# Encoder trunk on one core: ten warming products behind a memset of their own, and a weight's low part moved ahead of the last row sums' low parts

## The chip, the cores and the metric

The kernel runs on one core of one Trainium2 chip. The metric is the device time of one execution in microseconds (us). Before the change the median of three runs is 1899.04 us (1897.82, 1899.04 and 1899.11).

## What is computed

The reference is an encoder of two layers over 512 tokens of width 1024, in float32. Each layer adds three terms to the residual x, each computed from a root-mean-square norm of x:

```
x += 1/2 * SwiGLU(norm(x))                            feed-forward 1, inner width 2816
x += W_o( g_na * NA(h) W_na + g_f * FNet(h) W_f )     mixer, h = norm(x), gates g = sigmoid(h W + bias)
x += 1/2 * SwiGLU(norm(x))                            feed-forward 2
```

NA is attention with 8 heads of 64 over bands of keys with a relative bias; FNet is the real part of a 2-D Fourier transform of another projection of h. A last norm follows the second layer.

## The kernel before, in words

Every product is made in three matmuls on parts of the operands: a value is split into a high part, a rounded copy that ACT makes, and a low part, the value minus its high part, that DVE makes; then come high by high, high by low and low by high. Many large products are also cut into quarters by Strassen's scheme, so seven block products named 1 to 7 stand for eight.

**Weights.** They come as granules of 128x1024 floats, in an order written out in `stage_items`. `Stream` walks through them: a granule is fetched by a DMA of SP several places ahead (with a second, adding DMA of POOL for a summed quarter), and `prep` makes its parts. ACT copies `raw` into `whi` (line 178, or 173 with the sign turned), DVE subtracts to give `wlo` (line 181, or 174). `whi` and `wlo` have three buffers each. `ws.prep(to)` issues these for all granules up to `to`; `ws.next(ahead)` hands out the granule at `ws.pos` and prepares `ahead` more.

**The front.** Lines 129 to 135: DVE sets `ones` and `warm`, ACT runs one Tanh on `ones` so that its table is loaded, and writes the result into a column of `warm`; PE then runs `WARM` products of `warm` by itself, whose result nobody reads. They are followed by the first real block, `cl`: for each of eight tiles of the input, `given` (line 345 on) makes `xh` on ACT (L303), `xr` (L352) and `xl` (L304) on DVE from a tile `xt` that SP fetches and `gn` that ACT's queue fetches; PE multiplies by `whi` with `xh` and `xl` (L470, L471) for four blocks of tokens and then by `wlo` (L473).

**Attention's end.** In `stage_mixer` the order of DVE's and ACT's instructions is written out by hand (a `manual_schedule` block): each of the two engines keeps the order of the program text there, and PE's order is left to the scheduler outside of the inner blocks. At the end of the block stand the last two of eight attention steps, 6 and 7. `att_pv` makes their weighted sums on PE (`ps` from `p` and `v` or `vs`), `att_split` splits each sum into `o` (high on ACT, L1284; low on DVE, L1287), two instructions a step on each engine. The tile `o` of the last pair of heads is the last quarter of the contraction of the output product `fill(o, ns, 0, w)`: 48 matmuls at L294, L295, L296 that use two granules, called here the first and the second; `fill` runs three quarters of two row blocks before it needs the last quarter.

**What comes behind it.** The gates' first Strassen products are prepared in a second hand-ordered block. `minus` gives `t12` in three DVE steps: two differences (L1416) and their sum (L1418). ACT copies `t12` (`high`, L1641, tile t1h), then `ws.prep(ws.pos + 3)` makes the first granule of block product 1 (L173 on ACT, L174 on DVE). DVE goes on with L1416, t1l (L1646), two more additions into `t12` (L1656), L1416; ACT copies `t12` again (L1641, t2h), DVE makes t2l, and then comes the second granule of product 1 (L173, L174), the copies of `fill`'s results (L1313) and the granules of product 5 (L178, L181). PE runs product 1 into `A` (L470, L471, L473), then product 5 into `B`. Each engine takes its instructions strictly in its own order.

The stage occurs once in each of the two layers, with the same text.

Of the kernel before, what the change touches and what calls it, by code (L numbers as in the profile page):

```python
# [9 lines left out]
F32 = mybir.dt.float32  # L10
# [3 lines left out]
AF = mybir.ActivationFunctionType  # L14
# [3 lines left out]
P = 128  # L18
# [8 lines left out]
NH, DH = 8, 64  # L27
EPS = 1e-6
NEG = -1.0e30
WARM = 9  # L30
AHEAD = 2
ORDER = (1, 5, 2, 6, 7, 3, 4)
FETCH = 8
# [56 lines left out]
def encoder_kernel(  # L90
# [3 lines left out]
    V, S, G, PE = nc.vector, nc.scalar, nc.gpsimd, nc.tensor  # L94

    cp = ctx.enter_context(tc.tile_pool(name="cp", bufs=1))
    sp = ctx.enter_context(tc.tile_pool(name="sp", bufs=1))
# [8 lines left out]
    def nm(s):  # L106
        uid[0] += 1
        return f"{s}_{uid[0]}"

    def slot(dt=F32, s="k", shape=(4, 256)):  # L110
        return kp.tile([P, *shape], dt, tag="k", name=nm(s), bufs=23)

    def hilo(s):
        t = slot(F32R, s, (2, T))
        return t[:, 0, :], t[:, 1, :]

    def bank(s="ps"):
        return pp.tile([P, T], F32, tag="ps", name=nm(s))
# [7 lines left out]
    idents = cp.tile([P, 2, P], F32, tag="ident", name="ident")  # L126
    ident, mirror = idents[:, 0, :], idents[:, 1, :]
    ones = cp.tile([P, 1], F32, tag="ones", name="ones")
    V.memset(ones, 1.0)
    warm = slot(BF16, "warm", (T,))  # L130
    V.memset(warm, 0.0)
    S.activation(warm[:, 0:1], ones, AF.Tanh)
    pw = bank()
    for _ in range(WARM):
        PE.matmul(pw, warm[:, 0:P], warm, start=True, stop=True)
# [120 lines left out]
    class Stream:  # L256
# [27 lines left out]
        def next(self, ahead=AHEAD):  # L284
            self.prep(self.pos + 1 + ahead)
            it = self.items[self.pos]
            self.pos += 1
            return it.out

    ws = Stream()  # L290
    raw_pool = [None]

    def mm3(ps, lh, ll, rh, rl, start, stop, again=False):
        PE.matmul(ps, lh, rh, start=start, stop=False, skip_group_check=again)  # L294
        PE.matmul(ps, lh, rl, start=False, stop=False, skip_group_check=again)  # L295
        PE.matmul(ps, ll, rh, start=False, stop=stop, skip_group_check=again)  # L296
# [680 lines left out]
    def stage_mixer(l, norm, nxt):  # L977
# [288 lines left out]
        def att_pv(i, p_):  # L1266
            hp, pr = divmod(i, 2)
            po = bank()
            hs = slice(hp * P, (hp + 1) * P)
            for jj in range(2):  # L1270
                ph, pl = p_[jj]
                for c in range(2):
                    vh, vl = vch[BAND[2 * pr + jj] + 2 * c]
                    cs = slice(c * 256, (c + 1) * 256)
                    mm3(po[:, jj * 256 : jj * 256 + 256], vh[:, hs], vl[:, hs], ph[:, cs], pl[:, cs], c == 0, c == 1)
            return po

        def att_split(i, po):
            hp, pr = divmod(i, 2)
            pv = po.rearrange("p (a e q) -> p a e q", a=2, e=2)  # L1280
            oh, ol = [z[:, pr * 256 : pr * 256 + 256].rearrange("p (a q) -> p a q", a=2) for z in o[hp]]
            for e in range(2):
                r = slice(64 * e, 64 * e + 64)
                S.activation(oh[r], pv[r, :, e, :], AF.Copy)  # L1284
            for e in range(2):
                r = slice(64 * e, 64 * e + 64)
                V.tensor_tensor(ol[r], pv[r, :, e, :], oh[r].bitcast(F32), ALU.subtract)  # L1287


        def rows_of(src, tb, w, kts=range(4), ps=None):  # L1290

            ps = bank() if ps is None else ps
            t = slice(tb * P, (tb + 1) * P)
            for kt in kts:
                h_, l_ = src[kt]
                wh, wl = w[kt // 2]
                c = slice((kt % 2) * T, (kt % 2 + 1) * T)
                mm3(ps, h_[:, t], l_[:, t], wh[:, c], wl[:, c], kt == 0, kt == 3)
            return ps
# [112 lines left out]
        def minus(p, q, s):  # L1412

            t = [slot(F32, s), slot(F32, s)]
            for z in range(2):
                V.tensor_tensor(t[z], p[z], q[z], ALU.subtract)  # L1416
                yield t
            V.tensor_tensor(t[0], t[0], t[1], ALU.add)  # L1418
            yield t

        def f_copy(i, tb, ps, by_act=False):

            if tb % 2 == 0:
                fs[i, tb // 2] = slot(F32, "fs", (2, T))
            to = fs[i, tb // 2][:, tb % 2, :]
            if by_act:
                S.activation(to, ps, AF.Copy)
            else:
                V.tensor_copy(to, ps)

        first_f = []
        with tc.manual_schedule(engines={mybir.EngineType.DVE, mybir.EngineType.Activation}):
            with tc.manual_schedule(engines={mybir.EngineType.PE}):
# [179 lines left out]
                first = minus(B[0, 0], B[0, 1], "t1")  # L1613
# [14 lines left out]
                pt_[7] = [h() for h in ph]  # L1628
                ws.prep(ws.pos + 1)
                f_copy(1, 3, rows_of(yf, 3, second_f), True)  # L1630
                t12, _ = next(first)
                o.append(hilo("o"))
                po = [att_pv(i, pt_.pop(i)) for i in (6, 7)]
                att_split(6, po[0])
                att_split(7, po[1])
        ws.prep(ws.pos + 2)
        acts = {1: (hx[0], lx[0], 0), 2: (hx[1], lx[1], 0), 3: (hx[1], lx[1], 256), 4: (hx[0], lx[0], 256)}

        def high(src, s):
# [138 lines left out]
    for l in range(L):  # L1778
        nxt = Norm(3 * l + 1)
        stage_ffn(norm, nxt, False)  # L1780
        norm, nxt = nxt, Norm(3 * l + 2)
        stage_mixer(l, norm, nxt)
        norm, nxt = nxt, Norm(3 * l + 3)
        stage_ffn(norm, nxt, l == L - 1)
        norm = nxt
# [139 lines left out]
```

## Time and profile before

| what | value |
|---|---|
| median of the runs | 1899.04 us |
| the profiled execution's own time | 1898.17 us |
| its span, first to last instruction | 1896.4 us |
| time around the span | 1.77 us |
| TensorE clock granted, mean | 0.999 |
| DVE busy | 1647.8 us (87%) |
| ACT busy | 1189.4 us (63%) |
| DMA | 372.74 MB, mean 197 GB/s |

The profile is of one execution. In a row of the timeline the columns are the start (us from the span's start), the duration, engine, line, operation, tiles (output, then inputs), shape, and in brackets the idle time of the engine ahead of the instruction with what released it. PE stands for matmuls, PEld for the loads of their stationary operand, which overlap with the matmul before. A matmul's duration contains its filling and draining: what counts for a chain of matmuls is the distance from start to start.

### The profile page before, as it was taken

To read this page: it belongs to the slowest core of one execution; us is meant where nothing else is said; L and a number is where in the kernel's file an instruction comes from. 1 tells how busy PE (TensorE), PEld (TensorE's weight loads), DVE (VectorE), ACT (ScalarE), POOL (GpSimd) and SP (SyncE) were. 2 spreads that over 40 slices of the span, in tenths; PEclk is the share of its full clock that TensorE was granted. 3 is DMA by queue.
4 is the path that set the end of the run, shared out by engine and by line. 5 is a ranking of instruction groups with operands and counts; after the bars stand their busy time and mean duration, and the time that the engine had idled before them with its cause. 6 is when DMAs were issued, how large, how long until landed. Compare 5 with 4: busy or idle time off the path is not lost.

```text
span 1896.4 us, 25088 instructions
## 1 busy us (share of the span) xinstructions
PE 1884.2 (99%) x9149; PEld 1579.3 (83%) x9149; DVE 1647.8 (87%) x2006; ACT 1189.4 (63%) x1700; POOL 171.5 (9%) x210
## 2 busy tenths in 40 slices
PE   9999999999999999999999999999999999999998
PEld 7888888888888888888888888888888888888886
DVE  7877899788989977889997778998989899887898
ACT  6655665668666755566665556666685576556664
POOL 0101011100111011001010100101001101100010
PEclk9999999999999999999999999999999999999999
DMA  9777498932886777649877664988248767766594
GB/s 302 202 201 194 148 247 265 225 106 97 248 218 165 183 188 205 175 154 263 250 184 213 185 181 152 268 273 204 84 139 238 206 167 179 207 175 178 173 283 137
DMA packets 106939, 372.74 MB, mean 197 GB/s; under 512 B 12288, under 2 KB 12416, under 8 KB 106816
## 3 DMA queue, kind: packets, MB, share of 16 engines
q1 hardware_dynamic: 78144, 272.80, 41.9%
q0 software_dynamic: 28528, 98.33, 28.4%
q8 instruction: 71, 1.16, 0.2%
q14 instruction: 52, 0.43, 0.1%
q10 hardware_dynamic: 144, 0.02, 0.0%
HBM read 365.85 MB, written 2.11 MB: 194 GB/s over the span
## 4 chain that ended last, share of the span: by engine, by line
PE 98%; DVE 1%; issue 0%; ACT 0%; DVEq 0%; ACTq 0%
PE A L470 10%; PE A L471 10%; PE A L473 10%; PE o L470 7%; PE o L473 7%; PE o L471 7%; PE B L470 5%; PE B L471 5%; PE B L473 5%; PE ps L295 4%; PE ps L294 4%; PE ps L296 3%; PE C L471 2%; PE C L470 2%; PE C L473 2%; PE tr L593 2%
## 5 line engine op out<-in xcount | busy, mean ns | idle before, releaser
L178 ACT ACTIVATE whi<-raw 128x1024 fp32r<-128x1024 f32 (+1 forms) x536 | 553.6, 1037 | 387.1 <-PE A L471 123.4
L181 DVE TENSOR_TENSOR wlo<-raw,whi 128x1024 fp32r<-128x1024 f32 (+1 forms) x536 | 636.2, 1193 | 167.7 <-ACT whi L178 166.1
L149 POOL DMA_DIRECT2D raw<-in_wst_dram x166 | 144.4, 895 | 1375.5 <-DMA raw<-in_wst_dram 846.1
L163 DVE TENSOR_TENSOR raw<-raw,raw 128x1024 f32<-128x1024 f32 (+1 forms) x150 | 177.5, 1191 | 1.2
L471 PE MATMUL A<-whi,xl 128*128 128x512 f32 x400 | 155.7, 389 | 0.0
L470 PE MATMUL A<-whi,xh 128*128 128x512 f32 x400 | 155.7, 389 | 0.0
L473 PE MATMUL A<-wlo,xh 128*128 128x512 f32 x400 | 115.1, 389 | 0.0
L173 ACT ACTIVATE whi<-raw 128x1024 fp32r<-128x1024 f32 (+1 forms) x83 | 85.8, 1036 | 43.0 <-PE o L471 12.8
L174 DVE SCALAR_TENSOR_TENSOR wlo<-raw,whi 128x1024 fp32r<-128x1024 f32 (+1 forms) x83 | 98.0, 1195 | 13.1 <-ACT whi L173 13.1
L675 ACT ACTIVATE th<-sn,rh 128x512 f32<-128x512 f32 x80 | 56.9, 714 | 69.2 <-DVE sn L545 69.2
L540 ACT ACTIVATE sn<-A 128x512 f32<-128x512 f32 x104 | 60.7, 588 | 46.4 <-PE A L473 46.3
L473 PEld LDWEIGHTS A<-wlo,xh 128*128 128x128 f32 x400 | 75.1, 188 | 15.6
L471 PEld LDWEIGHTS A<-whi,xl 128*128 128x128 f32 x400 | 75.1, 188 | 15.4
L470 PEld LDWEIGHTS A<-whi,xh 128*128 128x128 f32 x400 | 75.1, 188 | 15.4
L470 PE MATMUL C<-whi,xh 128*128 128x512 f32 x208 | 81.1, 390 | 0.0
L471 PE MATMUL C<-whi,xl 128*128 128x512 f32 x208 | 81.0, 389 | 0.0
L471 PE MATMUL B<-whi,xl 128*128 128x512 f32 x208 | 81.0, 389 | 0.0
L470 PE MATMUL B<-whi,xh 128*128 128x512 f32 x208 | 80.9, 389 | 0.0
L473 PE MATMUL C<-wlo,xh 128*128 128x512 f32 x208 | 59.8, 389 | 0.0
L473 PE MATMUL B<-wlo,xh 128*128 128x512 f32 x208 | 59.8, 389 | 0.0
L470 PE MATMUL B<-whi,t5h 128*128 128x512 f32 x136 | 54.2, 399 | 0.0
L695 DVE TENSOR_TENSOR at<-at,at 128x1024 f32<-128x1024 f32 (+1 forms) x48 | 53.8, 1130 | 0.0
(446 smaller groups left out, 4783.9 us busy)
## 6 DMA issues: line engine op xcount, KB each, us to landing
raw<-in_wst_dram SPq DMA_DIRECT2D x470, 512.0 KB, 5.3
raw<-in_wst_dram POOLq DMA_DIRECT2D x174, 512.0 KB, 8.0
raw<-in_wst_dram SPq DMA_DIRECT2D x30, 256.0 KB, 3.9
bm<-in_bias_dram SPq DMA_DIRECT2D x16, 384.0 KB, 3.8
vs<-v SPq DMA_DIRECT2D x12, 256.0 KB, 3.8
x<-in_xin_dram SPq DMA_DIRECT2D x4, 512.0 KB, 10.2
raw<-in_wst_dram POOLq DMA_DIRECT2D x8, 256.0 KB, 8.1
dft<-in_dft_dram POOLq DMA_DIRECT2D x8, 256.0 KB, 4.2
```

The lines of the kernel that those rows point to most:

```text
L149: G.dma_start(out=self.t, in_=wst[GRAN_AT[self.plus]][:, 0 : self.n], accum_op=ALU.add)
L163: V.tensor_tensor(self.raw.t, self.raw.t, self.add.t, ALU.add)
L173: S.activation(hi, t, AF.Copy, scale=-1.0)
L174: self.last = V.scalar_tensor_tensor(lo, t, -1.0, hi.bitcast(F32), ALU.mult, ALU.subtract)
L178: S.activation(hi[:, cs], t[:, cs], AF.Copy)
L181: self.last = V.tensor_tensor(lo[:, cs], t[:, cs], hi[:, cs].bitcast(F32), ALU.subtract)
L294: PE.matmul(ps, lh, rh, start=start, stop=False, skip_group_check=again)
L295: PE.matmul(ps, lh, rl, start=False, stop=False, skip_group_check=again)
L470: PE.matmul(ps, lh, rh, start=start, stop=False, skip_group_check=again)
L471: PE.matmul(ps, ll, rh, start=False, stop=False, skip_group_check=again)
L473: PE.matmul(ps, lh, rl, start=False, stop=stop, skip_group_check=again)
L540: S.activation(t[:, b, :], ps[b], AF.Copy)
```

## The change

It has two parts.

- **Front.** `warm` is set first and `ones` second on DVE; ACT's Tanh writes into a small tile of its own instead of a column of `warm`; there are ten warming products instead of nine.
- **Attention's end.** The sum that finishes `t12` (L1418 on DVE) moves from ahead of steps 6 and 7 to behind their splits, as the last line of the hand-ordered block; and `ws.prep(ws.pos + 2)`, which makes the second granule of `fill`, moves from behind the block to a place ahead of the two splits and inside the block.

```diff
-WARM = 9
+WARM = 10
...
-    V.memset(ones, 1.0)
     warm = slot(BF16, "warm", (T,))
     V.memset(warm, 0.0)
-    S.activation(warm[:, 0:1], ones, AF.Tanh)
+    V.memset(ones, 1.0)
+    S.activation(sp.tile([P, 8], F32, tag="sq", name=nm("sq"), bufs=2)[:, 0:1], ones, AF.Tanh)
...
                 ws.prep(ws.pos + 1)
                 f_copy(1, 3, rows_of(yf, 3, second_f), True)
-                t12, _ = next(first)
                 o.append(hilo("o"))
                 po = [att_pv(i, pt_.pop(i)) for i in (6, 7)]
+                ws.prep(ws.pos + 2)
                 att_split(6, po[0])
                 att_split(7, po[1])
-        ws.prep(ws.pos + 2)
+                t12, _ = next(first)
```

The order of instructions on each engine that results, at attention's end (numbers count the granules):

```
DVE before: wlo 1 | L1418 | o x4 | wlo 2        | L174 | L1416 | t1l | L1656 x2 | L1416 | t2l | L174
DVE after:  wlo 1 | wlo 2 | o x4 | L1418        | L174 | L1416 | t1l | L1656 x2 | L1416 | t2l | L174
ACT, both:  whi 1 | fs | whi 2 | o x4 | t1h | L173 | t2h | L173 | L1313 x4 | L178 x2
```

On PE the 48 matmuls of `fill` change places among themselves: before, both `L294` of the third quarter and three matmuls of the third row block run ahead of the first use of wlo 2, the 18th matmul after the start; after, that use is the eighth matmul. The scheduler also exchanges some neighbours elsewhere: on ACT and DVE in the first feed-forward block of layer 0 and in the gates of both layers. SP's and POOL's orders are the same.

## Prediction

> **What bounds the kernel now.** I read the page first, then the waits of PE's weight loads, then the timeline around the two edited places.
>
> ```profile
> PE 1884.2 (99%) x9149; PEld 1579.3 (83%) x9149; DVE 1647.8 (87%) x2006; ACT 1189.4 (63%) x1700; POOL 171.5 (9%) x210
> ...
> PE 98%; DVE 1%; issue 0%; ACT 0%; DVEq 0%; ACTq 0%
> ```
>
> PE is busy 99% of the span and is 98% of the chain that ended last. Neither edit removes a real matmul, so only time in which PE stands still can be won, and only holes newly torn can be lost. The view of waits, taken for the weight loads, lists what there is:
>
> ```profile
> PEld L135 <- ACT warm L132: 2.7, 1, 2.7
> PEld ps L295 <- DVE wlo L181: 1.5, 4, 0.5
> PEld cl L471 <- DVE xl L304: 0.3, 1, 0.3
> ```
>
> The columns are total us, times, longest. The first row is the start of the kernel. The second is attention's end: four waits, two a layer, 0.23 and 0.53 us. The third is one wait right behind the front. All three matter below.
>
> **The front.** The timeline of the first 11 us:
>
> ```profile
> 0.81 0.06 DVE L129 MEMSET ones<- 128x1 f32 x1 [0.81 <-PEq L1914]
> 0.90 0.27 DVE L131 MEMSET warm<- 128x256 uint32 x1
> ...
> 2.73 4.02 PE L135 MATMUL ps<-warm 128*128 128x512 bf16 x9 [2.73 <-ACT warm L132]
> ...
> 4.81 0.61 ACT L178 ACTIVATE whi<-raw 128x512 fp32r<-128x512 f32 x1
> ...
> 8.57 0.73 ACT L303 ACTIVATE xh<-xt,gn 128x512 fp32r<-128x512 f32 x1 [2.31 <-DMA xt<-in_xtr_dram]
> ...
> 9.33 0.75 DVE L304 SCALAR_TENSOR_TENSOR xl<-xt,gn,xh 128x512 fp32r<-128x512 f32 x1
> ...
> 10.14 0.19 PEld L471 LDWEIGHTS cl<-whi,xl 128*128 128x128 f32 x1 [0.35 <-DVE xl L304]
> ```
>
> PE now starts at 2.73. After the change it needs only the memset of `warm`, which becomes DVE's first work: 0.81 + 0.27 + some 0.05 gives 1.13, 1.6 us earlier. Nine products take 4.02, so ten take about 4.45, and they end at 5.58 instead of 6.75. The first `whi` is there at 5.42, so the first real product follows at once, 1.17 earlier. But the second tile of the input lands by DMA at 8.57, `xh` is ready at 9.30, `xl` at 10.08, and the first matmul with that `xl` starts at 10.14 now, after a wait of its own. Nothing in the change moves that DMA, ACT's L303 or DVE's L304. The first tile's twelve matmuls fill 6.75 to 9.99 now (the chain's numbers, below) and at most as long after, so from 5.58 they are done by 8.8; PE then waits for `xl`, and at 10.14 it is where it was. **The front's value is 0.** The ACT write and the smaller memset lie under ACT's table load; POOL and SP do not wait on either.
>
> The chain of waits shows why the range is not zero. PE is slow at first:
>
> ```profile
> 6.75 0.43 PE cl L470
> ...
> 7.92 0.23 PE cl L471
> ...
> 9.99 0.23 PE cl L470
> ```
>
> A matmul takes 0.43 at 6.75 and 0.23 from 7.92 on, some 5 us after PE's start (the last of the warming products ends at 6.75, the first tile's twelve real ones at 9.99); had the switch come 2 us later, the first tile would have ended after 10.08, and PE would have lost time that the earlier start protects. The Trainium skill, "TensorE: Matmul & The Clock Gate", Part 1, says that the clock is let up after about 3.4 us of activity seen in a window that runs freely, so that the switch falls differently from run to run; the pace here agrees, the spread over runs cannot be seen in one trace. By that rule the front would win something in some runs; that is a rival below.
>
> **Attention's end, the gain.** Layer 0, in the order of time:
>
> ```profile
> 481.43 0.39 PE L296 MATMUL ps<-whi,o 128*128 128x512 f32 x1
> 481.93 0.50 PE L295 MATMUL ps<-wlo,o 128*128 128x512 f32 x1
> 482.27 0.39 PE L296 MATMUL ps<-whi,o 128*128 128x512 f32 x1
> ```
>
> Starts are 0.23 apart when nothing waits, as at the end of the chain's rows above. From 481.43 to 481.93 are 0.50, a loss of 0.27; then 0.34, a loss of 0.11, since the first matmul after a wait has its weight load uncovered. That wait is for the second `wlo`. Its place on DVE and the copy that it needs:
>
> ```profile
> 476.63 1.22 DVE L181 TENSOR_TENSOR wlo<-raw,whi 128x1024 fp32r<-128x1024 f32 x1
> 476.84 1.07 ACT L178 ACTIVATE whi<-raw 128x1024 fp32r<-128x1024 f32 x1
> ...
> 477.76 1.22 DVE L1418 TENSOR_TENSOR t<-t,t 128x1024 f32<-128x1024 f32 x1
> 477.79 1.55 ACT L1284 ACTIVATE o<-ps 64x256 fp32r<-64x256 f32 x4
> ...
> 477.90 0.50 PE L295 MATMUL ps<-wlo,o 128*128 128x512 f32 x1
> ...
> 478.90 1.72 DVE L1287 TENSOR_TENSOR o<-ps,o 64x256 fp32r<-64x256 f32 x4
> ...
> 479.37 1.06 ACT L1641 ACTIVATE t1h<-t 128x1024 fp32r<-128x1024 f32 x1
> 480.34 1.04 ACT L173 ACTIVATE whi<-raw 128x1024 fp32r<-128x1024 f32 x1
> ...
> 480.65 1.23 DVE L181 TENSOR_TENSOR wlo<-raw,whi 128x1024 fp32r<-128x1024 f32 x1
> 481.79 1.22 DVE L174 SCALAR_TENSOR_TENSOR wlo<-raw,whi 128x1024 fp32r<-128x1024 f32 x1
> ```
>
> After: wlo 2 starts when its `whi` is done (476.84 + 1.07 = 477.91, with the signal 477.97) and ends at 479.19. PE's new order asks for it as eighth matmul, from 477.90 about 479.4: covered, by 0.2. The four L1287 start at 477.97 + 1.14 = 479.11 (large DVE work follows at 1.14) and end near 480.9; PE needs them at about 482.4: covered. The first wait (477.90) stays, since wlo 1 doesn't move. **Gain: 0.27 + 0.11 = 0.38 a layer.**
>
> **Attention's end, the cost.** L1418 goes behind the four L1287: it starts at 479.11 + 1.75 = 480.86 and ends at 482.08, instead of 478.98. ACT's next instruction, t1h, reads that sum, so a new wait stands on ACT from 479.34 to 482.11. Queued behind it are L173, t2h, the second L173, L1313 and the L178s. L173 then starts at 483.08 instead of 480.34 and ends at 484.12, and DVE's L174, behind wlo 2 and L1418, waits for it: 484.18 instead of 481.79. **DVE is 2.39 later from there**, and it has no idle time to catch up in:
>
> ```profile
> 486.58 1.23 DVE L1656 TENSOR_TENSOR t<-t,xl 128x1024 f32<-128x1024 f32 x1
> ...
> 487.84 1.06 ACT L1641 ACTIVATE t2h<-t 128x1024 fp32r<-128x1024 f32 x1 [6.46 <-DVE t L1656]
> 488.80 1.05 ACT L173 ACTIVATE whi<-raw 128x1024 fp32r<-128x1024 f32 x1
> ...
> 490.07 1.22 DVE L174 SCALAR_TENSOR_TENSOR wlo<-raw,whi 128x1024 fp32r<-128x1024 f32 x1
> 491.80 2.03 ACT L178 ACTIVATE whi<-raw 128x1024 fp32r<-128x1024 f32 x2
> ...
> 491.81 0.39 PE L470 MATMUL A<-whi,xh 128*128 128x512 f32 x1
> ...
> 492.72 0.61 PE L473 MATMUL A<-wlo,xh 128*128 128x512 f32 x2
> ...
> 494.53 0.39 PE L470 MATMUL B<-whi,t1h 128*128 128x512 f32 x1
> ```
>
> ```profile
> 497.57 24.26 SPq L147 DMA_DIRECT2D raw<-in_wst_dram  x10
> ```
>
> From L174 at 481.79 DVE's work is one piece up to 491.29, L174's end; t2h follows the second L1656 and L173 follows t2h. All shift by 2.39: the second granule's `whi` is ready at 489.85 + 2.39 = 492.24, its `wlo` at 491.29 + 2.39 = 493.68. PE, 0.38 ahead, wants them at 491.43 and 492.34. It gets `whi` at 492.28: 0.85 lost, plus 0.11 for the first matmul after the wait. Its L473 would come at 493.30 and gets `wlo` at about 493.73: 0.43 more, plus 0.11. Together 1.50, less the gain of 0.38: **1.1 us slower a layer**; without the 0.11s, 0.9.
>
> What is next late is product 5. Its first `whi` (491.80 + 1.05 = 492.85) comes at 495.24; PE, now 1.1 late, wants it at 495.6: covered by 0.4. Product 1's first granule (484.12 and 485.40) is wanted only from 488.7. SP's order doesn't change; its next weight loads leave (497.57) when DVE's L181 has read a buffer, so they too come 2.4 later, for granules eight places ahead (`FETCH`). So the loss ends there. The exchanged neighbours in the gates and in the first feed-forward block lie where no wait of PE is listed and move single pieces of 0.2 to 1.2; I take 0, with 0.3 to either side. Layer 1 has the same spacing:
>
> ```profile
> 1422.42 0.19 PEld L295 LDWEIGHTS ps<-wlo,o 128*128 128x128 f32 x1 [0.53 <-DVE wlo L181]
> ...
> 1428.32 1.06 ACT L1641 ACTIVATE t2h<-t 128x1024 fp32r<-128x1024 f32 x1 [6.46 <-DVE t L1656]
> ...
> 1432.30 0.39 PE L470 MATMUL A<-whi,xh 128*128 128x512 f32 x1
> ```
>
> **Sum.** Front 0, two layers 2 x 1.1 = +2.2. The profiled execution took 1898.17 (its span 1896.4 and 1.77 around it): 1900.4. The median of the runs is 0.87 above that execution, 1899.04, which would give 1901.2; I take the middle, **1900.8**, with 1899.9 to 1901.7 as this case's own range (0.9 to 1.1 a layer, either base, 0.3 for the neighbours). From the middle base, 1898.6, the rivals are counted.
>
> **Rivals.**
>
> - *Only the wait goes.* ACT and DVE absorb the later L1418, for instance if PE asks for product 1's second granule later than it does now. Then 2 x 0.38 are won: 1897.8. For it speaks that the wait is the largest at this place; against it, that DVE's chain has no gap from 481.79 to 491.29 and that the second `whi` had 491.81 - 489.85, 1.96 us, to spare against 2.39 + 0.38. Chance 0.14.
> - *The clock's switch falls differently in each run.* Then the old start costs up to about 0.9 in some runs (a switch at 9.5 makes four more matmuls of the first tile slow, 0.2 each) and the new one never; 1899.9 together with the cost above. This is the skill's rule; the runs' spread of 1.3 us speaks for it, the profiled run, where the first tile ends just in time, neither way. Chance 0.14.
> - *Slower by over 0.2%: PE cools down.* PE now idles, in all some 1.3 us, between the first tile's end and 10.14, where it had 0.35. If that is enough for the pace to fall back, the next 5.2 us (2.73 to 7.92, what it took now) run at 0.43 instead of 0.23: 5.2 / 0.43 = 12 matmuls by 0.20, 2.4 us. With the 2.2: 1903.2. Against it: no gap of this length lies within the trace behind the start, so its effect isn't seen; PE is busy most of that window. Chance 0.05.
> - *The change doesn't do what it says.* wlo 2 now waits for a copy on ACT; were that 0.2 later, the eighth matmul would wait in place of the 18th and the 0.38 would not be won: 1901.6. Chance 0.05.
>
> **How the numbers follow.** The forecast holds 0.62. Its own range with the last rival's and the clock's holds about 0.75; to reach 0.8 the range goes down into the first rival's side and somewhat above: 1898.3 to 1902.2. Faster by over 0.2% (3.8 us, about what a measurement of this kernel can tell from no change) would be below 1895.2, and no case gets there: 0.02. Slower is above 1902.8: the cooling case and a rest, 0.06. Within: 0.92.
>
> **What would show it.** In the changed kernel's waits, the 0.53 at L295 is gone and two new ones a layer stand at product 1's second granule: `A` L470 for ACT's `whi` L173, about 0.8, and `A` L473 for DVE's `wlo` L174, about 0.4. ACT shows about 2.8 idle ahead of t1h, DVE about 2.1 ahead of L174. At the front PE starts at 1.1, and `cl` L471 with the second `xl` still starts at 10.1, after a wait of over 0.5. Wrong would be: no wait at `A`, an `xl` that comes earlier, or matmuls of 0.43 after 10.14.

## The result, and the profile after

| | before | after |
|---|---|---|
| median of 13 runs each, us | 1899.27 (1897.82 to 1902.27) | 1903.73 (1901.39 to 1904.71) |
| the profiled execution, us | 1898.17 | 1901.97 |
| its span, us | 1896.4 | 1899.9 |

The ratio is 1.0021, 95% interval [1.0013, 1.0029]: the changed kernel is slower by 4.0 us (2.5 to 5.5; the two medians alone lie 4.46 apart). The forecast, 1900.8 in a range of 1898.3 to 1902.2, lies below it.

PE's busy row and the chain's shares, from the page of the changed kernel:

```profile
PE 1884.8 (99%) x9150; PEld 1578.3 (83%) x9150; DVE 1647.3 (87%) x2006; ACT 1189.3 (63%) x1700; POOL 171.6 (9%) x210
...
PE 94%; issue 2%; DMA 2%; DVE 1%; SPq 0%; ACT 0%; POOL 0%; DVEq 0%; POOLq 0%; ACTq 0%
```

The work is the same; but the chain, which was PE for 98%, now holds 2% of DMA. The waits of the weight loads (total us, times, longest) say where:

```profile
PEld A L470 <- ACT sn L540: 4.2, 5, 2.3
PEld A L470 <- ACT whi L173: 2.2, 2, 1.1
...
PEld cl L470 <- ACT whi L178: 1.3, 2, 1.1
...
PEld B L470 <- ACT whi L178: 0.9, 2, 0.4
...
PEld cl L473 <- DVE wlo L181: 0.7, 1, 0.7
...
PEld ps L295 <- DVE wlo L181: 0.5, 2, 0.2
```

The 0.53 at L295 is gone, as forecast. The L173 row is the forecast wait. The first row is the surprise. Before, it read:

```profile
PEld A L470 <- ACT sn L540: 1.3, 5, 0.3
```

Attention's end in the timeline of layer 0:

```profile
475.65 2.54 DVE L181 TENSOR_TENSOR wlo<-raw,whi 128x1024 fp32r<-128x1024 f32 x2
...
476.92 0.19 PEld L295 LDWEIGHTS ps<-wlo,o 128*128 128x128 f32 x1 [0.24 <-DVE wlo L181]
...
478.11 1.74 DVE L1287 TENSOR_TENSOR o<-ps,o 64x256 fp32r<-64x256 f32 x4
...
479.88 1.23 DVE L1418 TENSOR_TENSOR t<-t,t 128x1024 f32<-128x1024 f32 x1
...
481.14 1.06 ACT L1641 ACTIVATE t1h<-t 128x1024 fp32r<-128x1024 f32 x1 [2.77 <-DVE t L1418]
...
483.18 1.23 DVE L174 SCALAR_TENSOR_TENSOR wlo<-raw,whi 128x1024 fp32r<-128x1024 f32 x1 [2.08 <-ACT whi L173]
...
491.29 0.19 PEld L470 LDWEIGHTS A<-whi,xh 128*128 128x128 f32 x1 [1.09 <-ACT whi L173]
...
494.32 0.19 PEld L470 LDWEIGHTS B<-whi,t1h 128*128 128x128 f32 x1 [0.43 <-ACT whi L178]
```

This is the forecast's chain up to PE's first wait: 2.77 idle on ACT, 2.08 on DVE, 1.09 at `A`. The second wait that it named, at `A` L473, isn't there; one at `B` stands in its place. Further on, in product 7, lies what it lacked. POOL's L183 is the adding DMA of `prep` that turns product 6's weight into product 3's (`then` in the code); ACT copies the result (L178), and between ACT's two copies of A (L540) that L178 stands. The changed kernel, then the kernel before:

```profile
504.91 0.85 POOL L183 DMA_DIRECT2D raw<-in_wst_dram  x1 [18.03 <-DVE wlo L181]
...
509.61 0.60 ACT L540 ACTIVATE sn<-A 128x512 f32<-128x512 f32 x1 [1.21 <-PE A L473]
...
511.46 1.06 ACT L178 ACTIVATE whi<-raw 128x1024 fp32r<-128x1024 f32 x1 [1.25 <-DMA raw<-in_wst_dram]
...
512.43 0.58 ACT L540 ACTIVATE sn<-A 128x512 f32<-128x512 f32 x1
...
513.06 0.19 PEld L470 LDWEIGHTS A<-whi,t3h 128*128 128x128 f32 x1 [1.19 <-ACT sn L540]
...
1447.04 0.85 POOL L183 DMA_DIRECT2D raw<-in_wst_dram  x1 [22.29 <-DVE wlo L181]
...
1454.67 1.06 ACT L178 ACTIVATE whi<-raw 128x1024 fp32r<-128x1024 f32 x1 [2.32 <-DMA raw<-in_wst_dram]
...
1456.26 0.19 PEld L470 LDWEIGHTS A<-whi,t3h 128*128 128x128 f32 x1 [2.26 <-ACT sn L540]
```

```profile
503.51 0.85 POOL L183 DMA_DIRECT2D raw<-in_wst_dram  x1 [16.38 <-DVE wlo L181]
...
510.60 1.06 ACT L178 ACTIVATE whi<-raw 128x1024 fp32r<-128x1024 f32 x1 [0.31 <-PE A L471]
...
512.20 0.19 PEld L470 LDWEIGHTS A<-whi,t3h 128*128 128x128 f32 x1 [0.25 <-ACT sn L540]
```

Count from attention's end, PE's wait at L295 (477.90 before, 476.92 after). POOL issues L183 at 25.61 before and 27.99 after: 2.38 later, DVE's whole lateness, for POOL waits for DVE's L181 of product 6. PE is only 0.90 later there (first L540 at 31.79 and 32.69). Before, ACT's L178 was released by PE, 7.09 behind the issue. After, the DMA has 7.09 + 0.90 - 2.38 = 5.61 to land, and it took 6.55 and 7.63: late by 0.94 and 2.02. PE's waits at L540 grew by as much, 0.25 to 1.19 and to 2.26.

### The profile page after: what moved, and what is told of

Same layout as the page of the kernel before. It is cut to its first block, busy times and chain, and to the rows that moved or that the text cites. A ratio compares the mean times of both kernels' runs of the same rounds, so it can differ in the third digit from the quotient of the medians.

```text
span 1899.9 us, 25092 instructions
## 1 busy us (share of the span) xinstructions
PE 1884.8 (99%) x9150; PEld 1578.3 (83%) x9150; DVE 1647.3 (87%) x2006; ACT 1189.3 (63%) x1700; POOL 171.6 (9%) x210
## 4 chain that ended last, share of the span: by engine, by line
PE 94%; issue 2%; DMA 2%; DVE 1%; SPq 0%; ACT 0%; POOL 0%; DVEq 0%; POOLq 0%; ACTq 0%
PE A L470 10%; PE A L471 10%; PE A L473 10%; PE o L470 7%; PE o L471 7%; PE o L473 7%; PE B L470 5%; PE B L471 5%; PE B L473 5%; PE ps L294 3%; PE ps L295 3%; PE ps L296 3%; PE C L471 2%; PE C L470 2%; PE C L473 2%
## 5 line engine op out<-in xcount | busy, mean ns | idle before, releaser
L178 ACT ACTIVATE whi<-raw 128x1024 fp32r<-128x1024 f32 (+1 forms) x536 | 553.6, 1037 | 385.6 <-PE A L471 126.9
L181 DVE TENSOR_TENSOR wlo<-raw,whi 128x1024 fp32r<-128x1024 f32 (+1 forms) x536 | 635.3, 1192 | 166.7 <-ACT whi L178 165.3
L470 PE MATMUL A<-whi,xh 128*128 128x512 f32 x400 | 155.9, 390 | 1.3 <-ACT whi L173 1.3
L473 PE MATMUL A<-wlo,xh 128*128 128x512 f32 x400 | 115.1, 389 | 0.0
L174 DVE SCALAR_TENSOR_TENSOR wlo<-raw,whi 128x1024 fp32r<-128x1024 f32 (+1 forms) x83 | 98.0, 1193 | 17.3 <-ACT whi L173 17.3
L173 ACT ACTIVATE whi<-raw 128x1024 fp32r<-128x1024 f32 (+1 forms) x83 | 85.8, 1036 | 40.4 <-PE o L471 12.8
L540 ACT ACTIVATE sn<-A 128x512 f32<-128x512 f32 x104 | 60.6, 590 | 48.2 <-PE A L473 48.1
L470 PEld LDWEIGHTS A<-whi,xh 128*128 128x128 f32 x400 | 75.1, 188 | 17.5 <-ACT whi L173 2.2
L473 PEld LDWEIGHTS A<-wlo,xh 128*128 128x128 f32 x400 | 75.1, 188 | 15.6
L470 PE MATMUL C<-whi,xh 128*128 128x512 f32 x208 | 81.1, 390 | 0.0
L470 PE MATMUL B<-whi,xh 128*128 128x512 f32 x208 | 80.9, 389 | 0.0
L473 PE MATMUL C<-wlo,xh 128*128 128x512 f32 x208 | 59.8, 389 | 0.0
L473 PE MATMUL B<-wlo,xh 128*128 128x512 f32 x208 | 59.8, 389 | 0.0
L470 PE MATMUL B<-whi,t5h 128*128 128x512 f32 x136 | 54.2, 399 | 0.0
```

Of the source, the lines that this page charges most:

```text
L173: S.activation(hi, t, AF.Copy, scale=-1.0)
L174: self.last = V.scalar_tensor_tensor(lo, t, -1.0, hi.bitcast(F32), ALU.mult, ALU.subtract)
L178: S.activation(hi[:, cs], t[:, cs], AF.Copy)
L181: self.last = V.tensor_tensor(lo[:, cs], t[:, cs], hi[:, cs].bitcast(F32), ALU.subtract)
L473: PE.matmul(ps, lh, rl, start=False, stop=stop, skip_group_check=again)
L540: S.activation(t[:, b, :], ps[b], AF.Copy)
```

## The experiments

The theory at the start: the late L1418, with ACT's strict order behind t1h, is the whole loss. It reaches PE at product 1, as forecast, and a second time through POOL's DMA, ACT's L178 and the copy L540. Rivals: the exchanged neighbours in the gates; the earlier weight; the front; something that only follows from the L540's own place.

A measure that is free of the front: PE's time from the first wait at L295 to the last quarter of the second gate block (the wait at `A` L470 on `t3h` there), worked out from each trace.

| kernel | layer 0 | layer 1 |
|---|---|---|
| before; before_again | 74.32; 74.29 | 74.25; 74.29 |
| front_only | 74.26 | 74.26 |
| after; after_again; after_third | 76.14; 77.27; 76.34 | 77.20; 76.22; 77.26 |
| attention_only | 77.22 | 78.99 |
| sum_late_only | 78.96 | 76.38 |
| weight_ahead_only | 74.09 | 74.33 |
| copy_behind_weight | 74.42 | 74.30 |
| copies_first | 76.78 | 74.80 |
| short_add_attention | 75.22 | 75.22 |
| short_add_before | 74.27 | 74.32 |
| best_of_all | 74.31 | 73.51 |

In copies_first and best_of_all this stretch holds two matmuls fewer than in the others (331 weight loads against 333), because the scheduler moves them behind its end. At 0.23 each, 0.46 has to be added to these two rows before they are compared. Outside of this stretch and of the front the change shows no effect: from the same kind of wait in the first block, near 52 us, to the first wait at L295 it is 425.5 to 425.6 us in the two executions of the kernel before and the three of the changed one, and from the end of the stretch in layer 0 to its start in layer 1 866.0 to 866.2. From its end in layer 1 to the end of the span it is 403.8 and 404.6 before, 403.6 to 404.1 after.

### The parts alone

**front_only**: the change without its part at attention's end.

```diff
-WARM = 9
+WARM = 10
...
-    V.memset(ones, 1.0)
     warm = slot(BF16, "warm", (T,))
     V.memset(warm, 0.0)
-    S.activation(warm[:, 0:1], ones, AF.Tanh)
+    V.memset(ones, 1.0)
+    S.activation(sp.tile([P, 8], F32, tag="sq", name=nm("sq"), bufs=2)[:, 0:1], ones, AF.Tanh)
```

> The front's edit alone, attention's end as before. Theory A (the second input tile's arrival decides, and it arrives at a different time in each execution: 8.57 us in the profile of before, 6.77 in that of the changed kernel): the time falls by 0 to 1.0 us against before, 0.5 in the middle; in the profile PE takes up the second tile as soon as its xl is there. Rival B (the edit itself moves the arrival forward): the second tile's copy L303 starts near 6.8 again and 1.0 us is won. Rival C (the forecast): it starts near 8.6 and nothing is won.

Measured: 1899.15 against 1899.19, ratio 0.9999 [0.9991, 1.0008]. The second tile's L303 and two waits of PE:

```profile
5.88 0.22 PEld L470 LDWEIGHTS cl<-whi,xh 128*128 128x128 f32 x1 [1.15 <-ACT whi L178]
...
7.04 0.73 ACT L303 ACTIVATE xh<-xt,gn 128x512 fp32r<-128x512 f32 x1 [0.69 <-DMA xt<-in_xtr_dram]
...
21.13 0.30 PEld L473 LDWEIGHTS cl<-wlo,xh 128*128 128x128 f32 x2 [0.70 <-DVE wlo L181]
```

No wait for `xl` at 10.1: the tile landed 1.5 earlier than in the profiled execution of before. Against that execution PE leads by 1.1 at 19.7 and by 0.8 from 23 on: the wait at 21 is for a `wlo` that DVE makes at the end of one unbroken piece of work. The interval, 1.7 faster to 1.5 slower, can't tell the three theories apart; B falls with before_again below, where L303 starts at 6.96 with the old front.

**attention_only**: the old front with the change's attention's end.

> Attention's end alone, front as before. Theory A (DVE and ACT run 2.4 us late from the late sum on, never catch up within the gates' first block, and the adding DMA that waits for a wlo is late by as much): PE waits of about 1.1 (A L470 for whi L173) and 0.4 (B L470) in each layer as in the changed kernel, and 1 to 3 us a layer at A L470 for ACT's L540; the time is 5 us above before, 4 to 7. Rival B (the forecast: only product 1's second granule is late): 2.2 above before. Rival C (the front's edit causes the third wait): no wait above 0.3 at A L470 for L540, 2 to 3 above before.

Measured: 1905.21 against 1899.19, ratio 1.0029 [1.0018, 1.004]. The two waits of product 7:

```profile
514.98 0.19 PEld L470 LDWEIGHTS A<-whi,t3h 128*128 128x128 f32 x1 [2.25 <-ACT sn L540]
...
1458.35 0.19 PEld L470 LDWEIGHTS A<-whi,t3h 128*128 128x128 f32 x1 [2.45 <-ACT sn L540]
```

The whole loss is attention's end. That it is 1.5 above the changed kernel is within the two intervals.

**weight_ahead_only**: the old front; only `ws.prep(ws.pos + 2)` moves.

```diff
                 po = [att_pv(i, pt_.pop(i)) for i in (6, 7)]
+                ws.prep(ws.pos + 2)
                 att_split(6, po[0])
                 att_split(7, po[1])
-        ws.prep(ws.pos + 2)
```

> Only the weight's preparation moves ahead of the splits; the sum L1418 stays ahead of it, where it was. Theory A (the late sum is the whole cost): the waits of 0.53 at L295 go, L174 on DVE keeps its time, no wait at A L470 for L173 or above 0.3 for L540; 0.5 to 0.8 us below before. Rival B (the weight's place itself pushes the row sums' low parts and what follows too late): a new wait of 0.3 or more at L296 or at A, and the time is that of before or above.

Measured: 1900.11 against 1899.19, ratio 1.0001 [0.9992, 1.001]. The wait of 0.53 at L295 becomes 0.36, where the expectation had it gone; there is no wait at L173. The weight's move costs nothing and wins nothing that can be measured.

**sum_late_only**: the old front, and the other half; L1418 goes behind the splits, the weight stays behind them too.

```diff
-                t12, _ = next(first)
...
                 att_split(6, po[0])
                 att_split(7, po[1])
-        ws.prep(ws.pos + 2)
+                ws.prep(ws.pos + 2)
+                t12, _ = next(first)
```

> Old front, the weight's low part left behind the splits, only the sum L1418 put behind it. Theory A (the late sum with ACT's order behind t1h is the whole loss, the weight's move is worth nothing measurable): waits at A L470 for whi L173 of 0.8 to 1.3 a layer and for the copy L540 of 1 to 2.5 a layer, time +4 to +6 on the kernel before, like attention_only. Rival B (weight's move and late sum together are needed, because wlo 2 ahead of the splits delays the splits and with them the sum): time within +2 and no wait above 0.5 at L173.

Measured: 1903.69 against 1899.62, ratio 1.0024 [1.0014, 1.0033].

```profile
493.03 0.19 PEld L470 LDWEIGHTS A<-whi,xh 128*128 128x128 f32 x1 [0.75 <-ACT whi L173]
...
516.06 0.19 PEld L470 LDWEIGHTS A<-whi,t3h 128*128 128x128 f32 x1 [2.45 <-ACT sn L540]
```

Theory A holds; the rival that needs the weight's move falls. (In layer 1 the waits at L540 are 1.06 and, in the second block, 0.64. The profiled execution took 1907.13, the most of its nine runs; layer 0's 78.96 holds a stretch of lowered clock, for which see the last section.)

**copy_behind_weight**: the change with the old front, and ACT's L173 put ahead of its copy of the late sum.

```diff
-            h1 = high(t12, "t1")
             ws.prep(ws.pos + 3)
+            h1 = high(t12, "t1")
```

> Attention's end as changed, but ACT prepares product 1's first granule (L173) ahead of the copy t1h, which waits for the late sum. Theory A (ACT's strict order behind t1h is what makes everything late): L173 and L174 keep the times they had, no wait at A L470 for L173, none above 0.3 for L540, and 0.5 to 0.8 us below before. Rival B (the late sum itself, through t1l, t12 and the second copy, makes DVE late): waits at A remain, 1 to 5 us above before.

Measured: 1899.34 against 1899.19, ratio 1.0 [0.9992, 1.0009].

```profile
513.22 0.19 PEld L470 LDWEIGHTS A<-whi,t3h 128*128 128x128 f32 x1 [0.75 <-ACT sn L540]
```

One exchange on ACT removes the loss: L1418 is as late as in the change, but product 1's first weight no longer stands behind its copy. The expected 0.5 to 0.8 below the kernel before is missed, and the trace shows why nothing is won: POOL's L183 leaves 25.83 behind attention's end here, PE is earlier by the 0.38 won at L295, the DMA does not land earlier, and the wait at L540 grows by 0.50 and 0.39.

### The missed cost by itself

**copies_first**: attention_only, with both copies of A put ahead of product 3's L178 on ACT.

```diff
                     with tc.manual_schedule(engines={mybir.EngineType.Activation}):
                         s2 = snap(pa)
+                        ws.prep(ws.pos + 3)
                         with_n(arg(s1, 0, 0), 0)
```

> Attention's end as in the change, the old front, and in the gates the two copies of A (L540) both put ahead of product 3's first whi (L178) on ACT. Theory A (the copy stood behind an L178 that waits for POOL's adding DMA): the waits at A L470 for L540 fall from 2.25 and 2.45 to about 0.25 each, those for whi L173 (1.1) and whi L178 (0.4) stay; L178 still waits for the DMA, some 2 us on ACT, and product 3 in B has enough lead, so no wait takes their place. Time about 3.5 to 4.5 us below attention_only, so +1.5 to +2.5 on the kernel before. Rival B (the copy is late because everything on ACT is late after the late sum): waits at L540 stay above 1 us a layer and the time stays at +4 to +6. Rival C (the loss only moves on): L540 free, but product 3 in B then waits some 2 us for its own whi; time at +4 to +6.

Measured: 1903.78 against 1899.62, ratio 1.0021 [1.0012, 1.003]. Theory A's time is missed. Layer 0:

```profile
511.83 0.19 PEld L470 LDWEIGHTS A<-whi,t3h 128*128 128x128 f32 x1 [0.20 <-ACT sn L540]
...
517.15 2.96 ACT L178 ACTIVATE whi<-raw 128x1024 fp32r<-128x1024 f32 x3 [2.61 <-DMA raw<-in_wst_dram]
...
520.64 1.06 ACT L300 ACTIVATE xh<-t 128x1024 fp32r<-128x1024 f32 x1 [0.53 <-DVE t L1683]
...
523.04 1.22 DVE L301 TENSOR_TENSOR xl<-t,xh 128x1024 fp32r<-128x1024 f32 x1
...
524.31 0.19 PEld L471 LDWEIGHTS A<-whi,xl 128*128 128x128 f32 x1 [2.16 <-DVE xl L301]
```

L540 is free, but L178 still waits for the DMA, and now the next block's `xh` and `xl` stand behind it: 2.16 at another place. In layer 1 nothing takes the place (74.80, with the two matmuls 75.26). So it isn't the copy that is dear but the weight that lands late: rival C in kind, though at `xl`, not at product 3's `whi`.

**short_add_attention** and **short_add_before**: attention_only and the kernel before with the L183 of the first gate block cut to 32 of 1024 columns; every engine keeps its order. Product 3 lacks most of one summand of its weight in both.

```diff
-                G.dma_start(out=t, in_=wst[GRAN_AT[self.then]][:, 0:n], accum_op=ALU.add)
+                G.dma_start(out=t[:, 0:(c := 32 if self.then[1:3] == ("gb", 0) else n)], in_=wst[GRAN_AT[self.then]][:, 0:c], accum_op=ALU.add)
```

> As attention_only, with every engine's order the same; the adding DMAs that POOL issues between products 6 and 3 of the first gate block (L183, two a layer) add 32 columns instead of 1024, so that product 3 lacks most of one summand. Theory A (what the forecast missed is that this DMA, issued 2.38 later after attention's end because DVE is late, no longer lands before ACT wants it for L178, 5.6 after the issue): with little to move it lands within 5 us, the waits at A L470 for the copy L540 fall from 2.25 and 2.45 to about 0.25, those for L173 (1.1) and for L178 at B (0.4) stay, from attention's end to the second block's copy PE needs 75.2 a layer (74.3 in before); time +1.5 to +2.2 on the kernel before. Rival B (fixed latency or POOL's queue, not the bytes): L178 still starts 6.5 to 7.8 after the issue, waits at L540 stay above 1, time +4 to +6. Rival C (DVE's lateness reaches PE by another way as well): L540 free, another wait of 1 to 2 within the first gate block, time above +3.

> The kernel before with the same short adding DMAs (product 3 of the first gate block lacks most of one summand). Theory A: ACT's L178 was released by PE there, 7.1 after the issue, so nothing changes: time within 0.7 of the kernel before, waits at L540 of 0.24 as before. If the DMA had a price in the kernel before as well, it is 1 or more faster.

Measured: 1900.55 against 1899.02, ratio 1.0011 [1.0002, 1.002]; and 1898.74 against 1899.02, ratio 0.9995 [0.9986, 1.0004]. From short_add_attention, the list of DMAs and the timeline:

```profile
raw<-in_wst_dram POOLq DMA_DIRECT2D x4, 16.0 KB, 3.0
```

```profile
505.16 0.85 POOL L183 DMA_DIRECT2D raw<-in_wst_dram  x1 [17.45 <-DVE wlo L181]
...
510.81 1.07 ACT L178 ACTIVATE whi<-raw 128x1024 fp32r<-128x1024 f32 x1 [0.31 <-PE A L471]
...
512.41 0.19 PEld L470 LDWEIGHTS A<-whi,t3h 128*128 128x128 f32 x1 [0.25 <-ACT sn L540]
```

The DMA is issued as late as in the change (27.99), but lands in 3.0, and ACT waits for PE again. What is left is 75.22 in both layers, 0.9 above before: the waits at `A` for L173 and at `B` for L178. This settles theory A: the DMA is the rest of the loss. Cutting it in the kernel before changes nothing that can be measured.

### A better version, and the spread

**best_of_all**: the whole change with the edits of copy_behind_weight and copies_first.

> The whole change, with ACT's sign-turned copy L173 ahead of its copy of the late sum (t1h), and with both copies of A ahead of product 3's L178. Theory A: no wait above 0.3 at L173, L178 and L540; beside copy_behind_weight the 0.75 and 0.63 at L540 go to about 0.25, some 0.9 won; the time is 0 to 1.5 below the kernel before, at the limit of what can be measured. Rival B: another wait takes the place of L540 (product 3 for its whi, or wlo L181): time within 0.5 of the kernel before or above it.

Measured: 1899.46 against 1899.62, ratio 1.0004 [0.9995, 1.0013]. With the two matmuls, layer 1's stretch takes 0.3 less than before, and 0.2 of that is lost again on the way to the wait at `wA` L470, 51 us on; in layer 0 the wait at `xl` (0.96) costs more than is won, much as rival B has it. No version here beats the kernel before by an amount that can be measured.

**before_again**, no edit:

> The kernel before, once more with a profile, to see what its trace repeats. If the second input tile's landing varies by execution, L303 of that tile starts near 6.9 and PE's wait for xl is gone; if it belongs to the old front, L303 starts at 8.57 again. ACT's L178 ahead of the copy L540 again starts about 7.1 after POOL issued its adding DMA, released by PE or by the DMA within 0.3, and L540 costs PE about 0.25 in each layer.

Measured: 1899.25.

```profile
6.96 0.73 ACT L303 ACTIVATE xh<-xt,gn 128x512 fp32r<-128x512 f32 x1
...
8.26 0.28 PEld L471 LDWEIGHTS cl<-whi,xl 128*128 128x128 f32 x1
...
8.57 0.19 PEld L470 LDWEIGHTS cl<-whi,xh 128*128 128x128 f32 x1
```

The late tile (8.57) belonged to one execution: in the other thirteen traces L303 starts at 6.66 to 7.33. ACT's L178 stood 7.10 behind POOL's issue again, released by PE, and L540 cost 0.24 and 0.25. The weight loads get shorter (0.28 to 0.19) when the clock is let up, here at 8.57 against 7.76 in the first profile.

**after_again**, **after_third**, no edit:

> The changed kernel once more, to see what the upper half of its runs holds: its profiled execution (1901.97) lies 1.8 below the median of its runs. Theory A (clock): when the adding DMA lands so late that PE's wait at L540 passes about 2.4 us, the granted clock falls to half for some 4 us behind it and 1.6 us more are lost; then an execution of 1903 or more has a stretch of granted clock below 0.7 behind a wait of over 2.4 at A L470, and one near 1902 has none. Theory B (plain spread): an execution of 1903 or more has no such stretch, and its extra time lies elsewhere. Either way the waits for L173 (1.1) and L178 at B (0.4) are there in both layers, and L178 starts 6.5 to 7.8 after POOL's issue.

> The same, a third execution, since which side it falls on is chance: theory A and B as for the second.

Measured: 1902.05 and 1902.59. No stretch of lowered clock is in either, and neither execution lies at 1903 or above, so these two traces don't decide between theories A and B. From L183's issue to L178 the DMA took 7.56 and 6.64, 6.73 and 5.94; with the two of the first profile, the lateness against 5.61 is 0.94, 2.02, 1.95, 1.03, 1.12 and 0.33, and the growth of the wait at L540 is 0.94, 2.01, 1.93, 1.01, 1.10 and 0.31.

## Why the prediction was wrong, step by step

- **Front, value 0.** About right in time, for the wrong reason. The lead of 1.17 at the first real product was 0.13 to 0.48 (it starts at 6.19 in the first profile of before and at 5.71 to 6.06 with the new front), because PE then waited 0.97 to 1.33 for ACT's first `whi`. The wait for `xl` at 10.1 was one execution's late tile. What differs goes with the clock's switch: with the old start, four executions in nine switched at 6.0 to 6.95 and five at 7.76 to 8.68. At a fixed point of the first block (the wait at `A` on `t3h` near 52 us) the first four stand at 51.62 to 51.74, the other five at 52.23 to 52.50; five with the new start stand at 51.42 to 51.66. So the rival *the clock's switch falls differently* was right in kind: by these traces the late switch costs the old start some 0.85 (52.40 less 51.55, the means), over all nine 0.5 (52.07 less 51.55); too little for front_only's interval to show. The spread agrees with the Trainium skill, "TensorE: Matmul & The Clock Gate", Part 1, which has the window run freely.
- **Attention's end, gain 0.38.** Right: the 0.53 went, the wait at 477.90 stayed.
- **The cost at product 1, net 1.1 a layer.** Right in kind, 0.90 in size. The wait for `whi` L173 came. That for `wlo` L174 did not: DVE had it ready at 492.69, 15.77 behind attention's end and so as late as forecast (493.68 less 477.90), but PE's order in product 1 has changed and asks for it 1.72 behind that wait instead of 0.91:

```profile
493.01 0.61 PE L473 MATMUL A<-wlo,xh 128*128 128x512 f32 x2
```

  So PE was at product 5 sooner, and 0.43 came there, at `B` for its first `whi`, which the forecast had "covered by 0.4".
- **The step that failed:** "SP's order doesn't change; its next weight loads leave (497.57) when DVE's L181 has read a buffer, so they too come 2.4 later, for granules eight places ahead (`FETCH`). So the loss ends there." It followed DVE's lateness to SP and not to POOL. POOL's L183 waits for the same engine, isn't eight places ahead, and its result is wanted 7.09 later. The page of before had a first sign of the price, the median from issue to landing of all of POOL's weight loads:

```profile
raw<-in_wst_dram POOLq DMA_DIRECT2D x174, 512.0 KB, 8.0
```

  The two that matter can be had from the same execution, with the list of DMAs cut to the stretch of each issue (503.4 to 504.6 and 1443.9 to 1445.1):

```profile
raw<-in_wst_dram POOLq DMA_DIRECT2D x1, 512.0 KB, 6.8
...
raw<-in_wst_dram POOLq DMA_DIRECT2D x1, 512.0 KB, 6.7
```

  They landed 0.3 and 0.4 ahead of the copy. With the 5.61 that are left after the change they would be 1.2 and 1.1 late, so the forecast could have had this term. It is 1.23 a layer as measured, the mean of the six lateness figures above. With 0.90 that makes 2.1, and with what the second gate block adds in some executions 2.46 (the mean of the table's six for the changed kernel, 76.74, less 74.28 for before, before_again and front_only). Two layers give 4.9, less 0.5 for the front 4.4, where the ratio gives 4.0 (2.5 to 5.5).
- **Exchanged neighbours, 0 within 0.3.** No run separates them, but the traces leave them little room: short_add_attention has those in the gates and loses only 0.9 a layer, and the two long stretches outside of it are the same within 0.2. One on PE, which the forecast didn't list, did count: the L473 above.
- **Rivals.** *Only the wait goes* fell. *The change doesn't do what it says* fell: wlo 2 came in time. *PE cools down* did not happen at the front, but see the last section.

## What to carry to other kernels

When an engine without idle time becomes late by d, go through every queue that one of its instructions releases, and compare for each the time from release to use with what the transfer takes; a queue whose margin is under d, less what the user of its result has become late itself, is a second loss, and it adds to the first. Look for the strict queue in which the late result is copied: whatever stands behind that copy is late as well, so the place in the queue, and not the engine, decides the price. And read a start from several executions before a wait in it is taken for a law.

## What the runs showed of the hardware

A long wait of PE costs more than itself. In attention_only, layer 1, the wait of 2.45 is followed by a stretch at a lower granted clock (the columns are the stretch, its length, PE busy with its matmuls, granted clock, DMA share, GB/s):

```profile
1453.00:1458.35 5.35, 3.32 (x16) 1.00 1.02 252
1458.35:1462.50 4.15, 4.15 (x11) 0.59 1.05 272
1462.50:1466.00 3.50, 3.50 (x17) 1.00 1.00 245
```

Some 4 us at 0.59 of the clock cost 1.6 (78.99 a layer, where layer 0 with a wait of 2.25 and no such stretch has 77.22, and 0.2 are the longer wait). The same followed the 2.45 in sum_late_only and a wait of 2.68 at `tr` L375 in weight_ahead_only, layer 1. It did not follow the waits of 2.25, 2.26, 2.18 and 2.16 in attention_only, after, after_again and copies_first. The Trainium skill, "TensorE: Matmul & The Clock Gate", Part 1, lets the clock fall after an idle window of about 3.4 us; none of these waits was that long, so here the measurement decides. What makes up the upper end of the changed kernel's runs (to 1904.71) stays open. None of its three profiled executions shows such a stretch. The three profiled executions that have one are listed with a mean granted clock of 0.998, those without one with 0.998 or 0.999; of the seven runs of the changed kernel above 1903 five are listed with 0.999, one with 0.998 and one with 0.997, which speaks against such stretches as the main cause.

The adding DMA of 512 KB (the first of the two in each layer's first gate block) took 5.9 to 7.8 us from POOL's issue to ACT's copy where the copy waited for it, in the changed kernel and attention_only; with 16 KB the median to landing was 3.0. Its time differs by 1.7 between executions of one kernel, and so does the loss that hangs on it.
